# One position bias, eight table look-ups: replicating bucket numbers over partitions in TensorE or through DRAM

## The chip, the cores and the metric

The kernel runs on one core of a Trainium2 chip. The metric is the time of one execution in microseconds of device time (us), as the median of several runs. TensorE multiplies matrices, VectorE and ScalarE work element by element, GpSimd does small work on the side, and SyncE (SP) issues all the transfers of this kernel.

## The reference

Two blocks of two layers each are run one behind the other on a sequence of 512 positions and a width of 1024. Only the first block has a position bias. Its sliding-window attention adds to each score of query q and key k a number that depends on the head and on a bucket of their distance:

```python
def t5_bucket(rel):
    n = jnp.maximum(rel, 0)
    max_exact = N_BUCKETS // 2
    nf = jnp.maximum(n, max_exact).astype(jnp.float32)
    large = max_exact + (jnp.log(nf / max_exact) / math.log(MAX_DISTANCE / max_exact)
                         * (N_BUCKETS - max_exact)).astype(jnp.int32)
    return jnp.where(n < max_exact, n, jnp.minimum(large, N_BUCKETS - 1))
...
    bucket = t5_bucket(pq[..., :, None] - pk[..., None, :])
    bias = rel_bias[bucket]
```

There are 32 buckets and 8 heads. The bias is computed once, and both layers of the first block use it. The rest of the reference (latent attention, a convolution branch, gates, MLPs, and the whole second block) is not touched by the change.

## The kernel before, in words

The program is written as Python generators, one for each piece of work. `weave` (L178) takes the next step of whichever generator is furthest behind its share, so the program order of a stage is a mixture of several pieces; the number given with each piece is the count of steps that it is taken to have. From that program order a planner makes the order of each engine's and of the SP queue's instructions before the run. On the chip each engine and SP then work through their own list in that order.

`prep_bias` (L387 to L462) runs once, in layer 0, woven in `mix_first` (L535 to L537) with the latent attention `mla` (36 steps), with `inputs` (projections, 13.7 steps) and with the convolution beside them. It is entered with BIAS_STEPS = 39.7 and has 38 steps. It has four parts:

1. The distances of 128 consecutive windows are formed and turned into bucket numbers by 15 comparisons on VectorE (L415). The result is cast to bf16 as `bkr` (L420): on partition p are the buckets of one distance pattern, 512 columns wide.
2. The bias table in DRAM, `biasD` (4 blocks, 8 heads, 128 queries, 256 keys), is filled with a large negative number (L410).
3. The 32 x 8 table of bias values is split in three bf16 parts `rb` (L427), so that three matmuls give it at full precision.
4. For i from 0 to 7 (L436) and j from 0 to 3, four matmuls (L442) each copy one row of `bkr` to 32 partitions of a PSUM tile: the stationary operand is one column of the identity, repeated 32 times. The tile is compared with the partition's bucket number. For even j VectorE does this in one operation (L451), for odd j ScalarE in two (L448, L449). The result is the one-hot `oh`, and three matmuls (L454) multiply it with the parts of the table into 32 partitions of `pb`, which is one of the two PSUM banks named "sc". After four j, ScalarE copies `pb` to SBUF (L457) and SP stores it with four transfers into the diagonals of `biasD` (L461).

The one-hot comes from the tag "y1" of 8 buffers, which the latent attention's operands use too, and the replicated tile from the bank named "m", of which there is one. The scores of `mla` (L740) take their banks from "sc" as well.

What stands around it: `load_w` (L211) loads a weight tile with one transfer on SP (L222) into one of two raw buffers, ScalarE rounds it (L223) and VectorE subtracts for the low part (L224); TensorE multiplies in triples (L230, L231, L232). `softmax_causal` (L761 to L775) runs on VectorE and ScalarE. When the stage is over, the window attention `swa` loads one block of the bias at a time (L790) into the tile "bias", and adds it to its scores (L796, L798) in the tile "S". "bias" and "S" have one buffer each.

Of the kernel before, what the change touches and what calls it, by code (L numbers as in the profile page):

```python
# [13 lines left out]
BF16 = mybir.dt.bfloat16  # L14
AF = mybir.ActivationFunctionType
ALU = mybir.AluOpType
# [4 lines left out]
P = 128  # L21
T = 512
# [5 lines left out]
class Build:  # L28
# [358 lines left out]
    def prep_bias(self):  # L387

        nc, A = self.nc, self.A

        ii = self.tl([P, 8, P], I32, "bias", "ii")
        pk, d = ii[:, 0:4], ii[:, 4:8]
        src = A["pos_pad"]
        nc.sync.dma_start(out=pk, in_=bass.AP(tensor=src.tensor, offset=src.offset,
                                              ap=[[1, P], [P, 4], [1, P]]))
        pq = self.sm("pq", 4, "pq", bufs=1, dt=I32)
        src = A["positions"]
        nc.sync.dma_start(out=pq, in_=bass.AP(tensor=src.tensor, offset=src.offset, ap=[[1, P], [P, 4]]))
        nc.gpsimd.tensor_tensor(out=d, in0=pq.unsqueeze(2).to_broadcast([P, 4, P]), in1=pk, op=ALU.subtract)
        fl = self.tl([P, 2, T], F32, "S", "nfbk")  # L400
        nf, bk = fl[:, 0], fl[:, 1]
        nc.vector.tensor_copy(out=nf, in_=d.rearrange("p b e -> p (b e)"))
        nc.vector.tensor_scalar(out=bk, in0=nf, scalar1=0.0, scalar2=16.0, op0=ALU.max, op1=ALU.min)

        self.biasD = self.dram.tile([4, 8, P, 256], F32, name="biasD")
        bd = self.biasD
        neg = self.ch("neg", n=256, tag="tmp")
        nc.gpsimd.memset(neg, NEG)
        for b in range(4):
            nc.sync.dma_start(out=bd[b].rearrange("h q k -> q h k"),  # L410
                              in_=neg.unsqueeze(1).to_broadcast([P, 8, 256]))
        yield
        for j in range(1, 16):
            th = math.ceil(16.0 * 8.0 ** (j / 16.0) - 1e-9)
            nc.vector.scalar_tensor_tensor(out=bk, in0=nf, scalar=float(th), in1=bk,  # L415
                                           op0=ALU.is_ge, op1=ALU.add)
            if j % 4 == 0:
                yield
        bkr = self.ch("bkr", BF16, tag="y1")
        nc.vector.tensor_copy(out=bkr, in_=bk)  # L420
        idr = self.sm("idr", P, "idr", bufs=1, dt=BF16)
        nc.vector.tensor_copy(out=idr, in_=self.ident)

        rb, rest = [], self.cvec("rbias")
        for k in range(3):
            rb.append(self.sm("rb", 32, "rb", bufs=3, dt=BF16))
            nc.vector.tensor_copy(out=rb[k], in_=rest)  # L427
            if k < 2:
                r = self.sm("rr", 32, "rr", bufs=2)
                nc.vector.tensor_tensor(out=r, in0=rest, in1=rb[k], op=ALU.subtract)  # L430
                rest = r
        yield
        nbk = self.sm("nbk", 1, "nbk", bufs=1)
        nc.vector.tensor_scalar(out=nbk, in0=self.cvec("bucket"), scalar1=-1.0, scalar2=None, op0=ALU.mult)

        for i in range(8):  # L436
            pb = self.psum("sc")
            for j in range(4):
                ps = self.psum("m")
                for g in range(4):  # L440
                    q = 32 * j + 8 * g + i
                    nc.tensor.matmul(ps[32 * g:32 * g + 32], idr[:, q:q + 1].to_broadcast([P, 32]), bkr,  # L442
                                     start=True, stop=True)
                oh = self.ch("oh", BF16, tag="y1")
                if j % 2:

                    t = self.ch("dd", tag="tmp")
                    nc.scalar.activation(out=t, in_=ps, func=AF.Square, bias=nbk)  # L448
                    nc.scalar.activation(out=oh, in_=t, func=AF.Relu, scale=-1.0, bias=self.ones[:, 0:1])  # L449
                else:  # L450
                    nc.vector.tensor_scalar(out=oh, in0=ps, scalar1=self.cvec("bucket"), scalar2=None,  # L451
                                            op0=ALU.is_equal)
                for k, w in enumerate(rb):
                    nc.tensor.matmul(pb[32 * j:32 * j + 32], w, oh, start=k == 0, stop=k == 2)  # L454
                yield
            ob = self.ch("ob", tag="tmp")
            nc.scalar.copy(out=ob, in_=pb)  # L457
            for b in range(4):
                dst = bass.AP(tensor=bd.tensor, offset=bd.offset + b * 8 * P * 256 + i * 257 + 1,
                              ap=[[8 * 257, 16], [P * 256, 8], [1, P]])  # L460
                nc.sync.dma_start(out=dst, in_=ob[:, b * P:(b + 1) * P])  # L461
        self.dump("bias", self.biasD)  # L462
# [1819 lines left out]
        "bias": 1, "S": 1}  # L2282
MOD_STEPS = 102, 70
CONV_RATE, SWA_STEPS, REST_STEPS = (0.3, 0.6, 1.45), 11.5, 18
IN_STEPS, BIAS_STEPS, CTX_STEPS = 13.7, 39.7, 12
RWB = dict(mm=3, lv=3, z=2)
GLA = dict(wide=1, ktok=1, gst=8, ghs=1, att=2, gw=4)
ODD_RATE, ODD_STEPS, OUT_STEPS = 4, 32, 40
# [223 lines left out]
```

## Time and profile before

| | |
|---|---|
| median of 3 runs | 3931.33 us (3928.62 to 3933.89) |
| profiled execution, its own time | 3927.74 us |
| its span | 3925.7 us |
| mean granted TensorE clock | 0.969 of full speed |
| TensorE busy | 3777.0 us |
| VectorE busy | 2397.6 us |
| ScalarE busy | 1741.0 us |
| GpSimd busy | 85.0 us |
| transfers on the queue of SP | 321.47 MB |

Busy time is the union of an engine's instructions. PE is the matmuls, PEld the weight loads that overlap them, DVE is VectorE, ACT ScalarE, POOL GpSimd, SP SyncE. Matmuls are pipelined, so one that is shown with 0.39 us may be followed by the next one after 0.23. A row of the timeline gives the start, the duration, the engine, the line, the operation and its operands.

### The profile page before, as it was taken

Reading aid. Unit: us, or ns where it says so; the run is one execution under the profiler, and the core shown is the slowest. Engines: PE = TensorE matmul, PEld = TensorE weight load, DVE = VectorE, ACT = ScalarE, POOL = GpSimd, SP = SyncE. Lnnn points to the kernel's source line nnn. Section 1 sums busy time; section 2 is a strip of 40 time slices with the busy share of each in tenths; the row PEclk is TensorE's granted clock in tenths of the full one; section 3 lists DMA queues with packets and bytes.
Section 4 is the critical chain, followed back from the end, with each engine's and each line's share of the span. In section 5 each row is a group of like instructions: output and inputs, shape, how many; then the busy total and the mean of one; then the engine's idle time right before and its main releaser. Section 6 shows DMA issues by size and latency. Waiting matters only on the chain.

```text
span 3925.7 us, 54880 instructions
## 1 busy us (share of the span) xinstructions
PE 3777.0 (96%) x21506; PEld 2970.5 (76%) x21506; DVE 2397.6 (61%) x4178; ACT 1741.0 (44%) x3923; POOL 85.0 (2%) x180
## 2 busy tenths in 40 slices
PE   8999999999999999999998999999999999889998
PEld 5566888886667888778885666688888887678887
DVE  7587567665786565657646566454444574756444
ACT  4655343334653333335537788432222264533332
POOL 0000000000000000000001000000000000000000
PEclk9999999999999999999998899899999999889999
DMA  3132345442132355531110000211111212012232
GB/s 129 49 92 83 101 155 180 157 143 65 56 94 85 121 166 171 187 116 45 45 43 2 2 2 2 76 56 64 65 65 65 83 50 68 6 59 95 97 97 75
DMA packets 115699, 324.98 MB, mean 83 GB/s; under 512 B 12528, under 2 KB 34032, under 8 KB 115440
## 3 DMA queue, kind: packets, MB, share of 16 engines
q1 hardware_dynamic: 115440, 321.47, 25.4%
q8 instruction: 169, 2.77, 0.3%
q14 instruction: 90, 0.74, 0.1%
HBM read 307.27 MB, written 12.58 MB: 81 GB/s over the span
## 4 chain that ended last, share of the span: by engine, by line
PE 79%; issue 11%; ACT 5%; DVE 4%; POOL 1%; DMA 0%; POOLq 0%; DVEq 0%; SPq 0%; ACTq 0%
PE ps_g L230 20%; PE ps_g L232 20%; PE ps_g L231 20%; PE ps_mm L1564 1%; PE ps_y L750 1%; ACT B L1621 1%; PE ps_sc L740 1%; PE ps_z L1531 1%; POOL r L308 1%; PE ps_y L825 1%; PE ps_sc L796 1%; PE ps_y L1236 1%; PE ps_lv L1611 1%; PE ps_sc L454 1%; PE ps_lv L1608 1%
## 5 line engine op out<-in xcount | busy, mean ns | idle before, releaser
L230 PE MATMUL ps_g<-hi,whi 128*128 128x512 f32 (+1 forms) x4464 | 1670.5, 374 | 21.2 <-ACT whi L223 13.7
L232 PE MATMUL ps_g<-hi,wlo 128*128 128x512 f32 (+1 forms) x4464 | 1654.9, 371 | 10.5 <-DVE wlo L224 10.4
L231 PE MATMUL ps_g<-lo,whi 128*128 128x512 f32 (+1 forms) x3744 | 1401.4, 374 | 2.3 <-DVE lo L954 1.8
L223 ACT CAST whi<-raw 128x1024 fp32r<-128x1024 f32 (+3 forms) x497 | 481.7, 970 | 1241.8 <-PE ps_g L231 1064.1
L230 PEld LDWEIGHTS ps_g<-hi,whi 128*128 128x128 f32 x4464 | 847.8, 190 | 190.2 <-ACT whi L223 23.8
L232 PEld LDWEIGHTS ps_g<-hi,wlo 128*128 128x128 f32 x4464 | 847.4, 190 | 166.4 <-DVE wlo L224 17.1
L231 PEld LDWEIGHTS ps_g<-lo,whi 128*128 128x128 f32 x3744 | 709.8, 190 | 135.0 <-issue 10.5
L224 DVE TENSOR_TENSOR wlo<-raw,whi 128x1024 fp32r<-128x1024 f32 (+3 forms) x497 | 557.2, 1122 | 165.7 <-ACT whi L223 160.0
L231 PE MATMUL ps_g<-x,whi 128*128 128x512 f32 (+1 forms) x720 | 253.1, 352 | 0.0
L1130 DVE SCALAR_TENSOR_TENSOR x<-ps_g,mod,x 128x512 f32<-128x512 f32 (+1 forms) x192 | 127.0, 662 | 200.3 <-PE ps_g L232 200.1
L879 DVE SCALAR_TENSOR_TENSOR macc<-mraw,cs,macc 128x1024 f32<-128x1024 f32 x140 | 175.7, 1279 | 6.8 <-DMA mraw<-in_mod_w 6.5
L638 DVE SCALAR_TENSOR_TENSOR cv<-u,taps,cv 128x512 f32<-128x512 f32 x240 | 177.1, 744 | 1.1
L1109 DVE TENSOR_SCALAR r<-ps_g 128x512 f32<-128x512 f32 x96 | 57.6, 602 | 180.3 <-PE ps_g L232 180.2
L231 PEld LDWEIGHTS ps_g<-x,whi 128*128 128x128 f32 x720 | 138.5, 192 | 16.5 <-issue 1.6
L589 DVE TENSOR_TENSOR x<-ps_g,x 128x512 f32<-128x512 f32 x64 | 44.2, 690 | 137.8 <-PE ps_g L232 137.8
L473 DVE TENSOR_TENSOR o<-ps_g,R 128x512 f32<-128x512 f32 x76 | 52.2, 689 | 114.6 <-PE ps_g L232 111.7
L1110 ACT ACTIVATE r<-r 128x512 f32<-128x512 f32 x96 | 53.4, 557 | 145.3 <-DVE r L1109 145.3
L308 POOL TENSOR_TENSOR r<-v,mhalf 128x4 f32<-128x4 f32 (+2 forms) x30 | 38.5, 1284 | 2792.5 <-DVE v L327 2135.6
L582 DVE SCALAR_TENSOR_TENSOR r<-ps_g,R 128x512 f32<-128x512 f32 x64 | 44.0, 688 | 80.9 <-PE ps_g L232 77.0
L204 DVE TENSOR_TENSOR lo<-r,hi 128x512 fp32r<-128x512 f32 x96 | 57.6, 600 | 40.7 <-ACT hi L203 40.7
L1621 ACT COPY B<-ps_lv 32x64 f32<-32x64 f32 x384 | 77.5, 202 | 6.4
L291 ACT ACTIVATE sq<-x 128x512 f32<-128x512 f32 (+1 forms) x91 | 49.1, 543 | 70.1 <-DVE x L1130 34.7
(508 smaller groups left out, 4574.3 us busy)
## 6 DMA issues: line engine op xcount, KB each, us to landing
raw<-in_l_mlp_w SPq DMA_DIRECT2D x128, 512.0 KB, 3.5
mraw<-in_mod_w SPq DMA_DIRECT2D x96, 512.0 KB, 4.5
raw<-in_w_in SPq DMA_DIRECT2D x82, 512.0 KB, 3.4
raw<-in_w_up SPq DMA_DIRECT2D x64, 512.0 KB, 3.5
raw<-in_w_down SPq DMA_DIRECT2D x64, 512.0 KB, 3.5
raw<-in_l_w_in SPq DMA_DIRECT2D x50, 512.0 KB, 3.5
raw<-in_w_branch SPq DMA_DIRECT2D x48, 256.0 KB, 2.8
bias<-biasD SPq DMA_DIRECT2D x16, 512.0 KB, 3.9
```

What stands on the lines that cost most here:

```text
L204: nc.vector.tensor_tensor(out=lo, in0=src, in1=hi.bitcast(F32), op=ALU.subtract)
L223: nc.scalar.copy(out=hi, in_=raw)
L224: nc.vector.tensor_tensor(out=lo, in0=raw, in1=hi.bitcast(F32), op=ALU.subtract)
L230: t.matmul(ps, w[0], x[0], start=start, stop=False)
L231: t.matmul(ps, w[0], x[1], start=False, stop=False)
L232: t.matmul(ps, w[1], x[0], start=False, stop=stop)
L308: self.nc.gpsimd.tensor_tensor(out=r, in0=v, in1=self.mhalf[:, :v.shape[1]], op=ALU.pow)
L638: nc.vector.scalar_tensor_tensor(out=y, in0=u[:, j:j + T], scalar=taps[:, c * 31 + j:c * 31 + j + 1], in1=y, op0=ALU.mult, op1=ALU.add)
L879: nc.vector.scalar_tensor_tensor(out=acc[s], in0=rw, scalar=self.cs[:, k, s:s + 1], in1=acc[s], op0=ALU.mult, op1=ALU.add)
L1109: nc.vector.tensor_scalar(out=t, in0=ps[s][:, :n], scalar1=0.0, scalar2=None, op0=ALU.max)
L1130: nc.vector.scalar_tensor_tensor(out=xx[c], in0=ps[:, :n], scalar=md[:, s, 5, c:c + 1], in1=xx[c], op0=ALU.mult, op1=ALU.add)
L1621: nc.scalar.copy(out=B[rows, :, j, :], in_=blocks(ps[rows, 0:64]))
```

## The change

The buckets `bkr` are stored to DRAM once. In each turn i, four loads bring rows of them back, each row spread over 32 partitions, into one tile `oh` of 128 partitions and 4 x 512 columns. The tile alternates between the tags "S" and "bias". One VectorE operation turns all of it into the one-hot in place. Twelve matmuls follow, the table's part as the outer loop and the column tile j as the inner one. The generator yields after the loads, after the comparison and after the matmuls, so it has 30 steps in place of 38; BIAS_STEPS goes from 39.7 to 31. The copy of `pb` and the four stores stay as they are.

```diff
         bkr = self.ch("bkr", BF16, tag="y1")
         nc.vector.tensor_copy(out=bkr, in_=bk)
-        idr = self.sm("idr", P, "idr", bufs=1, dt=BF16)
-        nc.vector.tensor_copy(out=idr, in_=self.ident)
+        bkD = self.dram.tile([P, T], BF16, name="bkD")
+        nc.sync.dma_start(out=bkD, in_=bkr)
...
         yield
-        nbk = self.sm("nbk", 1, "nbk", bufs=1)
-        nc.vector.tensor_scalar(out=nbk, in0=self.cvec("bucket"), scalar1=-1.0, scalar2=None, op0=ALU.mult)
 
         for i in range(8):
+            oh = self.tl([P, 4, T], BF16, ("S", "bias")[i % 2], "oh")
+            for j in range(4):
+                src = bass.AP(tensor=bkD.tensor, offset=bkD.offset + (32 * j + i) * T,
+                              ap=[[8 * T, 4], [0, 32], [1, T]])
+                nc.sync.dma_start(out=oh[:, j], in_=src)
+            yield
+            nc.vector.tensor_scalar(out=oh, in0=oh, scalar1=self.cvec("bucket"), scalar2=None, op0=ALU.is_equal)
+            yield
             pb = self.psum("sc")
-            for j in range(4):
-                ps = self.psum("m")
-                for g in range(4):
-                    q = 32 * j + 8 * g + i
-                    nc.tensor.matmul(ps[32 * g:32 * g + 32], idr[:, q:q + 1].to_broadcast([P, 32]), bkr,
-                                     start=True, stop=True)
-                oh = self.ch("oh", BF16, tag="y1")
-                if j % 2:
-
-                    t = self.ch("dd", tag="tmp")
-                    nc.scalar.activation(out=t, in_=ps, func=AF.Square, bias=nbk)
-                    nc.scalar.activation(out=oh, in_=t, func=AF.Relu, scale=-1.0, bias=self.ones[:, 0:1])
-                else:
-                    nc.vector.tensor_scalar(out=oh, in0=ps, scalar1=self.cvec("bucket"), scalar2=None,
-                                            op0=ALU.is_equal)
-                for k, w in enumerate(rb):
-                    nc.tensor.matmul(pb[32 * j:32 * j + 32], w, oh, start=k == 0, stop=k == 2)
-                yield
+            for k, w in enumerate(rb):
+                for j in range(4):
+                    nc.tensor.matmul(pb[32 * j:32 * j + 32], w, oh[:, j], start=k == 0, stop=k == 2,
+                                     skip_group_check=True)
+            yield
             ob = self.ch("ob", tag="tmp")
             nc.scalar.copy(out=ob, in_=pb)
...
-IN_STEPS, BIAS_STEPS, CTX_STEPS = 13.7, 39.7, 12
+IN_STEPS, BIAS_STEPS, CTX_STEPS = 13.7, 31, 12
```

## Rows read from the trace of the kernel before

**Rows 1.** The page's busy line: engine, busy us, share of the span, instructions.

```profile
PE 3777.0 (96%) x21506; PEld 2970.5 (76%) x21506; DVE 2397.6 (61%) x4178; ACT 1741.0 (44%) x3923; POOL 85.0 (2%) x180
```

**Rows 2.** Windows, layer 0 and 1: us; PE, PEld, DVE, ACT, POOL busy; clock, DMA.

```profile
66.10:253.10 187.00, 183.33 (x798) 102.50 (x796) 122.91 (x264) 112.15 (x267) 0.00 (x0) 0.98 0.20 58
940.90:1089.30 148.40, 141.95 (x580) 96.98 (x579) 112.24 (x252) 87.00 (x228) 0.00 (x0) 0.95 0.17 57
```

**Rows 3.** Groups of instructions, stage of layer 0: count | busy, mean ns | idle before.

```profile
L230 PE MATMUL ps_g<-hi,whi 128*128 128x512 f32 x122 | 54.0, 442 | 1.2 <-ACT whi L223 1.2
...
L454 PE MATMUL ps_sc<-oh,rb 128*32 128x512 bf16 x96 | 26.4, 382 | 0.8 <-ACT oh L449 0.8
...
L442 PE MATMUL ps_m<-bkr,idr 128*32 128x512 bf16 x124 | 15.8, 389 | 0.5 <-ACT dd L448 0.5
...
L451 DVE TENSOR_SCALAR oh<-ps_m,cv 128x512 bf16<-128x512 f32 x16 | 11.9, 746 | 10.6 <-PE ps_sc L454 8.8 <-PE ps_m L442 1.8
...
L449 ACT ACTIVATE oh<-dd,ones 128x512 bf16<-128x512 f32 x16 | 11.6, 725 | 0.8 <-PE ps_sc L454 0.6
L448 ACT ACTIVATE dd<-ps_m,nbk 128x512 f32<-128x512 f32 x16 | 11.0, 690 | 5.5 <-PE ps_m L442 5.4
```

**Rows 4.** The same groups, stage of layer 1 (940.9 to 1089.3 us).

```profile
L230 PE MATMUL ps_g<-hi,whi 128*128 128x512 f32 x122 | 53.3, 437 | 0.9 <-ACT whi L223 0.9
```

**Rows 5.** The chain of waits in the stage of layer 0 (66.1 to 253.1 us).

```profile
by line: PE ps_g L230 18.4%; PE ps_g L231 17.1%; PE ps_g L232 16.2%; PE ps_sc L454 12.3%; PE ps_y L750 10.5%; PE ps_sc L740 10.0%; PE ps_m L442 5.6%; PE ps_tr L745 5.6%; ACT pr L771 0.8%; ACT kh L732 0.7%; ACT whi L223 0.6%; ACT pT L747 0.4
```

**Rows 6.** Timeline of TensorE's matmuls, 75.9 to 77.7 us: start, duration.

```profile
75.88 0.40 PE L442 MATMUL ps_m<-bkr,idr 128*32 128x512 bf16 x4
76.21 0.50 PE L232 MATMUL ps_g<-hi,wlo 128*128 128x512 f32 x1
...
76.87 0.82 PE L454 MATMUL ps_sc<-oh,rb 128*32 128x512 bf16 x3
77.62 0.50 PE L231 MATMUL ps_g<-lo,whi 128*128 128x512 f32 x1
```

**Rows 7.** Timeline of TensorE's matmuls, 225.3 to 225.6 us.

```profile
225.36 0.39 PE L454 MATMUL ps_sc<-oh,rb 128*32 128x512 bf16 x1
225.37 0.40 PE L442 MATMUL ps_m<-bkr,idr 128*32 128x512 bf16 x3
225.59 0.60 PE L454 MATMUL ps_sc<-oh,rb 128*32 128x512 bf16 x2
```

**Rows 8.** Groups of VectorE by form, 30 to 70 us.

```profile
L224 DVE TENSOR_TENSOR wlo<-raw,whi 128x1024 fp32r<-128x1024 f32 x3 | 3.7, 1217 | 0.0
...
L384 DVE TENSOR_SCALAR ang<-ang 128x512 f32<-128x512 f32 x1 | 0.4, 417 | 0.0
```

**Rows 9.** Transfers: KB, us to landing; queue from 14.9 to 24 us; issue durations of L461.

```profile
raw<-in_w_qup SPq DMA_DIRECT2D x12, 128.0 KB, 2.0
...
biasD<-neg SPq DMA_DIRECT2D x4, 1024.0 KB, 8.5
...
q1 hardware_dynamic: 3337, 2.90, 99.9%
...
L461 SPq DMA_DIRECT2D biasD<-ob x32: 518/597/764, 89.3 to 231.5; - x32
```

**Rows 10.** Waits of SP, 55 to 235 us: total, times, longest.

```profile
SPq L222 <- DVE wlo L224: 61.9, 10, 11.1
```

**Rows 11.** The replications, over the whole run: ns min/median/max, first and last start.

```profile
L442 PE MATMUL ps_m<-bkr,idr x128: 376/389/609, 63.2 to 226.0; 128*32 128x512 bf16 x128
```

**Rows 12.** Timeline of VectorE at 49.5 us.

```profile
49.50 0.15 DVE L662 TENSOR_SCALAR bh<-cv 128x4 f32<-128x4 f32 x1
```

**Rows 13.** Timeline of SP at 232 us.

```profile
232.18 0.52 SPq L790 DMA_DIRECT2D bias<-biasD  x1
```

## The prediction

> **What bounds the kernel now.** I read the page's busy line first, to see which engine the whole run hangs on: TensorE is busy 96% of the span, VectorE 61%, ScalarE 44% [rows 1]. TensorE time that is removed can therefore come off the end, and time on the others mostly cannot. An average does not tell that of one stage, so the windows come next. The bias is built only in layer 0, beside the latent attention; the stage from the first score matmul (L740) to the first window score (L796) is 187.0 us long there, with TensorE busy 183.3 us. The same stage of layer 1, which builds no bias, takes 148.4 us [rows 2]. Its other work is the same (122 first products at L230 in both [rows 3, 4]), so this kernel contains its own control: the bias costs **38.6 us** of that stage. The lines of the stage say on what: 96 look-ups (L454) for 26.4 us, 124 of the 128 replications (L442) for 15.8 us, on VectorE 16 one-hots (L451) for 11.9 us, on ScalarE 32 more passes (L448, L449) for 22.6 us [rows 3]. The chain of waits agrees on where it hurts: L454 holds 12.3% and L442 5.6% of the stage's 187.0 us, 23.0 and 10.5, in sum **33.5 us**, and the one-hots are not among its large shares [rows 5].
>
> **What the edit saves.** All 128 replications go, with their 10.5 us of chain. The 96 look-ups stay 96 matmuls, but in eight groups of 12 over four column tiles in turn, in place of 32 groups of three on one tile. Three on one tile hold the next product back for 77.62 - 76.87 = 0.75 us; four replications on four tiles only for 76.21 - 75.88 = 0.33 us [rows 6]. So tiles overlap. Replications share one moving operand though, and the new look-ups bring four. The trace shows that too: one look-up, moving the one-hot, starts at 225.36 and three replications, moving the buckets, at 225.37, and the next look-up on the first tile comes at 225.59 as if it were alone [rows 7]. Two moving operands ran at once. I therefore price 12 as three rounds, like three in a row: 0.75 us, times 8 = **6.0 us** put back; the other end is all in series, 12 x 0.25 = 3.0 us, times 8 = 24.
>
> Against the chain this leaves 33.5 - 6.0 = 27.5 us; against the control 38.6 - 6.0 = 32.6. I take **27.5**, because eight ScalarE copies (L457), the one-hots and all the DMA of the bias remain in layer 0, and layer 1 has none of it.
>
> **What it puts in, and what hides it.**
> VectorE: 16 one-hots out of PSUM (11.9 us) become eight of 128x2048 from SBUF to SBUF. No row has that form. The nearest is the SBUF-to-SBUF scalar operation L384, 0.417 us for 512 columns, so at most four times that, 1.7 us; the ends are 0.42 and, by the two-input subtraction L224 at 1.22 us for 1024, 2.4 us [rows 8]. I take 1.7, 13.6 us in all. VectorE then carries 122.9 - 11.9 + 13.6 = 124.6 us in a stage of 187.0 - 27.5 = 159.5: 35 us idle hide it. ScalarE loses 22.6 us of 112.2 and needs no cover. The two small VectorE operations that go (the bf16 identity, the negated bucket) and the second score bank that comes free earlier count for nothing of their own: the control has both already.
>
> SP: one store and 32 loads are new. The bias stores L461, also issued four at a time, took 0.60 us each [rows 9]: 2.4 us for the four of a look-up, 19 us in all. SP has room, since it stood 61.9 us waiting at L222 for a weight buffer alone [rows 10]. Behind these issues stand the weight loads and the stores of the bias. The store of the buckets also waits for the cast L420, and the first load for the store to land; at 2.0 us for 128 KB that holds SP once, before the place of the first replication, with two weight buffers to draw on. Each later load waits for the matmuls that read its tile two turns before; those are long done. Cost on the path: nothing, at worst the 2.4 us of one set of issues for each look-up, 19 us, if SP were late with weights all eight times.
>
> The wait that is new is VectorE's, for the four loads. Behind it on VectorE stand the low halves of the weights (L224), which TensorE needs, and the softmax reductions. A 128-row load of 1 KB a row, the shape of each new one, lands in 2.0 us; the 1 KB rows that fill the bias in DRAM are the slow end, 8.5 us [rows 9]. The last of four is issued 1.8 us after the first, so it lands after 3.8 to 10.3 us. The weave gives cover: the 32 groups of replications start from 63.2 to 226.0 us [rows 11], one step of prep_bias each 163 / 31 = 5.3 us; with 31 steps in place of 39.7 over the shortened stage that is 5.3 x 39.7 / 31 x 159.5 / 187 = 5.8 us. Covered at 3.8, 4.5 us short at 10.3. But the queues do not keep the program's order: a preparation of the layer norm that the program reaches only after the bias (L662) runs at 49.50 us [rows 12], so the one-hot can come up on VectorE sooner than a step later. I take the near row, 2.0 us, and no exposed wait. At the far end eight waits of 10.3 us, 82 us, are more than the idle 35; that is the rival on the other side.
>
> The end of the bias: its last store is issued at 231.5 us [rows 9] and the first load of it at 232.18 [rows 13], some 21 us before the first window scores, which end the stage at 253.1 [rows 2]. prep_bias ends at step 30 of 31 in place of 38 of 39.7, the same place; this margin covers one longer look-up.
>
> **The sum.** The profiled execution took 3927.7 us (span 3925.7 and 2.0 around it), 3.6 below the median of the runs, 3931.3. 3927.7 - 27.5 = 3900.2, and on the scale of the median **3904**.
>
> **Rivals.**
> *Loads crowd onto few engines.* Each new load's source has an outer dimension of only 4 (the other 32 rows repeat). If its packets then use four of the 16 DMA engines, four loads put 128 packets on each of these. While the bias was filled, 2.90 MB took 99.9% of 16 engines for 9.1 us, 145.5 us of engine time, so one engine needs 51 ns for a KB [rows 9]: 6.5 us, and with the 2.0 of a landing 8.5. Past a step of 5.8 us that is 2.7 us of VectorE wait eight times, 22 us; without cover 68 us; midway 45 us, somewhat above the idle 35. I let a quarter of it, 11 us, come through to TensorE, which has a product or two queued: 3915. For it: the pattern in the diff. Against: two buffers let SP load early, and the waiting stays off TensorE in part.
> The Trainium skill's page "DMA: Bandwidth & Descriptors", section "Why a DMA increments its semaphore by 16 and not by 1", says that a transfer is spread over the largest number of engines up to 16 that divides the slowest dimension of both sides, here 4. By this rule the time is 3915, by the nearest row 3904; the rows above are of transfers whose outer dimension is 16 or 128, so the trace of before neither supports nor denies it.
>
> *The column tiles do not overlap* (the change does not do what it says). 24 us are put back: 33.5 - 24 = 9.5 us gained, 3922. The two moving operands at 225.4 us speak against it [rows 7].
>
> *The gain is lost elsewhere.* A new order on every queue, or the softmax, takes it. The control, which has the softmax without the bias, speaks against it: about 3931.
>
> *Slower: VectorE becomes the bound.* It stands in order at each one-hot with L224 behind it. The stage is as long as before once 124.6 + 8w = 187.0, at a wait w of 7.8 us for each look-up. At the far end w is 10.3 and the stage 124.6 + 82 = 207 us, 20 longer: 3951. For it: 8.5 us has been seen. Against: that was with 1 MB transfers in a row, and it needs no cover at all.
>
> **Chances.** Forecast 0.55, few engines 0.27, no overlap 0.05, lost 0.08, slower 0.05. The forecast's own range goes from 38.6 gained (3893) to about 20 (3911); the few-engines case from 3911 to 3920; **3893 to 3920** over both leaves out the no-overlap case, the lost, the slower, and the edges. About 0.2%, 8 us, is what a measurement of this kernel can tell: the first three cases are faster, 0.87; lost is the same, 0.08; slower 0.05.
>
> **What would show it.** In the changed profile: no L442; groups of 12 look-ups that hold the next product for 0.75 us (2 or more: no overlap); a stage of about 160 us between the first L740 and L796; a one-hot of 0.4 to 2.4 us. VectorE's wait for the loads should be under 2 us each; 3 to 8 us and landings of 7 or more mean few engines. The forecast is wrong if the stage stays over 175 us, and wrong in its reason if the stage shrinks and gives the time back before the first window scores, waiting for the bias.

## The result, and the profile after

The changed kernel took **3967.74 us** (median of 4 runs, 3963.77 to 3970.83), the kernel before 3930.62 beside it: ratio 1.0099, 95% interval 1.0085 to 1.0113. The forecast was 3904 and the range ended at 3920: the change is slower where I expected it to be faster. The profiled execution took 3963.77 us, its span is 3961.9.

The busy line of the page and the two windows of [rows 1, 2], now for the kernel after (stage of layer 0, then of layer 1; columns as there):

```profile
PE 3780.7 (95%) x21378; PEld 2966.7 (75%) x21378; DVE 2391.9 (60%) x4168; ACT 1721.3 (43%) x3891; POOL 85.6 (2%) x180
```

```profile
64.70:262.30 197.60, 167.43 (x678) 105.74 (x678) 118.09 (x260) 93.89 (x237) 0.00 (x0) 0.86 0.27 77
967.30:1113.50 146.20, 139.84 (x580) 95.38 (x579) 112.31 (x252) 87.03 (x228) 0.00 (x0) 0.98 0.18 58
```

TensorE has 128 instructions fewer in the run and is busy 3.7 us *longer* than in [rows 1]. In the stage with the bias it is busy 15.9 us less than in [rows 2], and the stage is 10.6 us longer all the same: idle time went from 187.0 - 183.3 = 3.7 us to 197.6 - 167.4 = 30.2, and the mean granted clock from 0.98 to 0.86. The layer-1 control is close to what it was (148.4 and 146.2 us). So the work did leave, and something worse came. The groups of the stage and its chain of waits say what:

```profile
L441 DVE TENSOR_SCALAR oh<-oh,cv 128x2048 bf16<-128x2048 bf16 x8 | 6.0, 753 | 34.2 <-DMA oh<-bkD 24.8 <-DMA raw<-in_w_kup 5.2 <-DMA raw<-in_w_qup 4.3
L446 PE MATMUL ps_sc<-oh,rb 128*32 128x512 bf16 x96 | 7.3, 413 | 0.0
```

```profile
by line: DMA oh<-bkD 17.5%; PE ps_g L230 10.2%; PE ps_g L232 10.1%; PE ps_g L231 10.0%; PE ps_y L743 9.3%; SPq L439 6.7%; PE ps_sc L733 5.8%; SPq L454 5.2%; PE ps_tr L738 4.8%; DMA raw<-in_w_kup 2.9%; PE ps_sc L446 2.7%; DMA raw<-in_w_qup 2
```

The 96 look-ups fell from 26.4 us busy [rows 3] to 7.3. The eight one-hots take 0.75 us each. But VectorE stands 34.2 us in front of them, and the loads lead the chain with 17.5%, where [rows 5] had no transfer at all. One of the eight episodes, in the timeline of all engines (start, duration, engine, line; in brackets the idle time before and what ended it):

```profile
98.73 2.68 SPq L439 DMA_DIRECT2D oh<-bkD  x4
...
109.83 0.75 DVE L441 TENSOR_SCALAR oh<-oh,cv 128x2048 bf16<-128x2048 bf16 x1 [5.31 <-DMA oh<-bkD]
110.50 0.16 DVE L766 RECIPROCAL rec<-sum 128x1 f32<-128x1 f32 x1
110.69 0.61 ACT L767 ACTIVATE pr<-pr,rec 128x384 f32<-128x384 f32 x1 [5.11 <-DVE rec L766]
...
111.36 0.90 PE L738 MATMUL ps_tr<-ident,pr 128*128 128x128 f32 x3 [4.99 <-ACT pr L767]
```

The loads are issued at 98.73 and the one-hot can start at 109.83, 11.1 us later. A reciprocal of the softmax (L766) stands behind it on VectorE, ScalarE waits for that, and TensorE for ScalarE. Over the whole stage (65 to 262 us), this last wait is the longest of TensorE's (total, times, longest), 18.5 of its 30.2 us of idle time:

```profile
PE ps_tr L738 <- ACT pr L767: 18.5, 7, 5.3
```

The windows around the episode (columns as in [rows 2]):

```profile
98.70:103.70 5.00, 4.98 (x22) 3.15 (x21) 4.05 (x11) 2.69 (x8) 0.00 (x0) 1.00 0.26 76
103.70:106.70 3.00, 2.67 (x21) 1.42 (x19) 0.82 (x3) 1.23 (x3) 0.00 (x0) 1.00 0.97 146
106.70:108.70 2.00, 0.00 (x0) 0.00 (x0) 0.00 (x0) 0.00 (x0) 0.00 (x0) 1.00 0.46 103
108.70:111.70 3.00, 0.34 (x2) 0.35 (x3) 1.87 (x4) 0.99 (x2) 0.00 (x0) 0.51 0.26 92
111.70:115.70 4.00, 1.35 (x5) 0.65 (x3) 3.25 (x8) 3.90 (x10) 0.00 (x0) 0.50 0.27 90
```

The DMA share is 0.26 while the loads run alone, about four of 16 engines (from 103.7 to 106.7 us a weight load, issued at 103.20, runs beside them), and once TensorE has stood still from 106.7 us its granted clock is 0.5 (1.2 GHz) from 108.7 on, so the matmuls after the wait are slow as well.

That is a quarter of the loss. The first window score (L789) comes at 262.29 instead of 253.1 us, 9 us late; the end comes 36 us late. The other 27 us are there when the second block begins. They build up evenly through the rest of the first block, 1,500 us in which nothing was edited: the first product of macc and sel starts at 590.15 us before and 606.56 after, 16.4 us late, and the first product of x, where the second block begins, at 1737.02 and 1776.07, 39.1 late. The second block adds nothing (36.2 late at its end). There is no wait there; the matmuls themselves follow each other more slowly. TensorE's timeline in the layer-0 MLP, before and then after, eight gaps each:

```profile
599.70 0.39 PE L230 MATMUL ps_g<-hi,whi 128*128 128x512 f32 x1
...
601.52 0.39 PE L232 MATMUL ps_g<-hi,wlo 128*128 128x512 f32 x1
```

```profile
599.70 0.40 PE L231 MATMUL ps_g<-lo,whi 128*128 128x512 f32 x1
...
601.56 0.40 PE L230 MATMUL ps_g<-hi,whi 128*128 128x512 f32 x1
```

1.82 us against 1.86, at a granted clock of 1.00 in both. Over all neighbouring products between 600 and 900 us the median distance is 0.227 us before and 0.235 after; the whole MLP stretch takes 404.5 and 415.4 us, filled with matmuls in both. What differs is where the tiles lie: the change drops two small tiles, idr (256 bytes) and nbk (32), from the pool at the bottom of the first block's memory, and every tile allocated behind them moves down by 288 bytes. By the allocation of the programs as built, weights begin 96 bytes into a 128-byte line in both kernels; the moving operands begin at 96 before and at 64 after.

### The profile page after: what moved, and what is told of

The parts are those of the page before. It is cut to its first block, busy times and chain, and to the rows that moved or that the text cites. A ratio compares the mean times of both kernels' runs of the same rounds, so it can differ in the third digit from the quotient of the medians.

```text
span 3961.9 us, 54607 instructions
## 1 busy us (share of the span) xinstructions
PE 3780.7 (95%) x21378; PEld 2966.7 (75%) x21378; DVE 2391.9 (60%) x4168; ACT 1721.3 (43%) x3891; POOL 85.6 (2%) x180
## 4 chain that ended last, share of the span: by engine, by line
PE 77%; issue 11%; ACT 5%; DVE 4%; POOL 1%; DMA 1%; SPq 1%; POOLq 0%; DVEq 0%; ACTq 0%
PE ps_g L230 20%; PE ps_g L232 20%; PE ps_g L231 20%; PE ps_mm L1557 1%; PE ps_y L743 1%; ACT B L1614 1%; DMA oh<-bkD 1%; POOL r L308 1%; PE ps_z L1524 1%; PE ps_sc L733 1%; PE ps_y L818 1%; PE ps_sc L789 1%; PE ps_y L1229 1%; PE ps_g L2152 1%; PE ps_lv L1604 1%
## 5 line engine op out<-in xcount | busy, mean ns | idle before, releaser
L230 PE MATMUL ps_g<-hi,whi 128*128 128x512 f32 (+1 forms) x4464 | 1678.5, 376 | 22.1 <-ACT whi L223 14.6
L232 PE MATMUL ps_g<-hi,wlo 128*128 128x512 f32 (+1 forms) x4464 | 1663.8, 373 | 12.1 <-DVE wlo L224 11.9
L230 PEld LDWEIGHTS ps_g<-hi,whi 128*128 128x128 f32 x4464 | 847.5, 190 | 196.3 <-ACT whi L223 25.2
L232 PEld LDWEIGHTS ps_g<-hi,wlo 128*128 128x128 f32 x4464 | 846.6, 190 | 180.5 <-DVE wlo L224 21.5
L224 DVE TENSOR_TENSOR wlo<-raw,whi 128x1024 fp32r<-128x1024 f32 (+3 forms) x497 | 557.4, 1122 | 165.7 <-ACT whi L223 160.9
```

Of the source, the lines that this page charges most:

```text
L224: nc.vector.tensor_tensor(out=lo, in0=raw, in1=hi.bitcast(F32), op=ALU.subtract)
L230: t.matmul(ps, w[0], x[0], start=start, stop=False)
L232: t.matmul(ps, w[1], x[0], start=False, stop=stop)
```

## The experiments

Two theories, then: the loads of the buckets are carried by four engines and land late; and the operands' addresses slow every first-block product. Each was undone alone, then both. All ratios are to runs of the kernel before on the same chip in the same session. "Stage" is the window from the first recorded latent score to the first window score (66.5 to 253.1 us before, 0.4 shorter than in [rows 2]), "L230" the mean duration of that product between 500 and 890 us.

| run | median us | ratio (95%) | stage us, clock | L230 ns |
|---|---|---|---|---|
| before | 3930.62 | 1 | 186.6, 0.98 | 391 |
| after | 3967.74 | 1.0099 (1.0085 to 1.0113) | 197.6, 0.86 | 397 |
| e1 after, 32-byte tile | 3939.63 | 1.0012 (0.9997 to 1.0027) | 191.8, 0.89 | 391 |
| e2 after, 64-byte tile | 3970.09 | 1.0090 (1.0073 to 1.0107) | 191.6, 0.89 | 397 |
| e3 before, 32-byte tile | 3962.62 | 1.0069 (1.0053 to 1.0085) | 186.3, 0.99 | 397 |
| e4 loads over 16 engines | 3943.71 | 1.0023 (1.0007 to 1.0038) | 165.7, 0.93 | 397 |
| e5 e4 and 32-byte tile | 3907.32 | 0.9952 (0.9937 to 0.9967) | 165.1, 0.93 | 391 |
| e6 e4, weights shifted | 3906.51 | 0.9955 (0.9939 to 0.9971) | 164.6, 0.93 | 391 |
| e7 before, 64-byte tile | 3937.51 | 1.0034 (1.0023 to 1.0045) | 185.9, 0.99 | 393 |
| e8 before, 12 look-ups | 3910.0 | 0.9953 (0.9937 to 0.9969) | 169.7, 0.97 | 391 |
| e9 e5, look-ups in series | 3911.27 | 0.9965 (0.9953 to 0.9977) | 163.5, 0.94 | 391 |
| e10 e5, second block moved | 3907.7 | 0.9954 (0.9937 to 0.9971) | 163.2, 0.95 | 391 |
| e11 e5, look-ups in threes | 3915.53 | 0.9952 (0.9934 to 0.9970) | 166.7, 0.96 | 392 |
| e12 e5, nine more look-ups | 3916.21 | 0.9972 (0.9961 to 0.9983) | 171.7, 0.98 | 391 |

### Addresses: e1, e2, e3

```diff
+        pad = self.sm("pad", 8, "pad", bufs=1)
+        nc.gpsimd.memset(pad, 0.0)
```

This stands at the head of prep_bias, in the kernel after (e1), there with 16 columns in place of 8 (e2), and in the kernel before (e3).

> The kernel after, with one more 32-byte tile ahead of the first block's tiles, so that every later tile of that block lies 32 bytes higher, as far into a 64-byte line as in the kernel before (the change took out two small tiles, 288 bytes together). Theory A (addresses): about 27 of the 37 us lost come from matmuls whose moving operand begins on a multiple of 64 bytes and that then follow each other every 0.2333 us instead of every 0.2268 us; the pad takes them back: 3938 to 3944 us, and the L230 matmuls of the layer-0 MLP have a mean of about 391 ns again. Rival B (order of work or the clock behind the bias stage is the cause): no change, 3964 to 3971 us and a mean of about 397 ns. Both: the bias stage itself stays at about 197 us with some 34 us of VectorE waits for the loads.

> The control of the run above: a 64-byte tile instead of the 32-byte one. Everything is moved, but the addresses stay as they are within a 64-byte line. Theory A (addresses modulo 64): no change, 3964 to 3971 us, L230 in the layer-0 MLP at about 397 ns. Rival (any extra tile and its memset, or addresses in some larger unit): as the 32-byte run, 3938 to 3944 us.

> The kernel before with the same 32-byte tile and nothing else: its first block's moving operands then begin on multiples of 64 bytes. Theory A: the loss without the change, 3955 to 3962 us, with the matmuls of the layer-0 MLP at 0.233 us and L230 there at about 397 ns. Rival B: 3928 to 3934 us.

All three came out as the address theory has it, with two small misses: e3 ended 0.6 us above its range, and the stage of e1 took 191.8 us where about 197 was expected. The group of L230 between 500 and 890 us, in the kernel after, in e1 and in e3:

```profile
L230 PE MATMUL ps_g<-hi,whi 128*128 128x512 f32 x543 | 215.6, 397 | 0.0
```

```profile
L230 PE MATMUL ps_g<-hi,whi 128*128 128x512 f32 x558 | 218.1, 391 | 0.0
```

```profile
L230 PE MATMUL ps_g<-hi,whi 128*128 128x512 f32 x541 | 214.9, 397 | 0.0
```

An unused tile of 32 bytes makes the kernel after 0.87% faster (1.0099 to 1.0012, 34 us), one of 64 bytes does nothing, and the same 32 bytes make the kernel **before** 0.69% slower with no other edit. So this loss has nothing to do with how the bias is computed: it came with two tiles that were no longer needed.

### Loads: e4, and both mends: e5

```diff
-            for j in range(4):
-                src = bass.AP(tensor=bkD.tensor, offset=bkD.offset + (32 * j + i) * T,
-                              ap=[[8 * T, 4], [0, 32], [1, T]])
-                nc.sync.dma_start(out=oh[:, j], in_=src)
+            for g in range(4):
+                src = bass.AP(tensor=bkD.tensor, offset=bkD.offset + (8 * g + i) * T,
+                              ap=[[0, 32], [32 * T, 4], [1, T]])
+                nc.sync.dma_start(out=oh[32 * g:32 * g + 32], in_=src)
```

The same rows go to the same places, in as many transfers of as many bytes; only the repeat of 32 is now the outermost dimension, ahead of the four rows.

> The kernel after with each of the four loads filling 32 partitions by four tiles instead of 128 partitions by one tile from a source that repeats in the middle; the data are the same. Theory C (the loads are carried by four of the sixteen DMA engines, and this makes them land late): with the repeat outermost all engines carry them, the loads land in 2 to 4 us, VectorE's waits for oh fall from 34 us to under 10, the bias stage from 197.6 to 160 to 172 us with its clock back above 0.93, and the time to 3932 to 3945 us (the addresses are left as in the kernel after). Rival D (the landing is late because of the queue's order or the issue on SP, or the stage is long for another reason): the landing stays above 6 us and the time at 3960 to 3970 us.

The packet counts tell of the engines, if each transfer adds one small packet per engine that takes part. Before, after and e4, first line of the DMA part of each page:

```profile
DMA packets 115699, 324.98 MB, mean 83 GB/s; under 512 B 12528, under 2 KB 34032, under 8 KB 115440
```

```profile
DMA packets 120066, 329.29 MB, mean 83 GB/s; under 512 B 12672, under 2 KB 38400, under 8 KB 119808
```

```profile
DMA packets 120450, 329.29 MB, mean 84 GB/s; under 512 B 13056, under 2 KB 38784, under 8 KB 120192
```

Under 512 B the kernel after has 144 more than before, 16 for the store and 32 x 4 for the loads; e4 has 528 more, 16 + 32 x 16. The Trainium skill's rule, cited in the prediction, that the slowest dimension sets the number of engines (page "DMA: Bandwidth & Descriptors", section "Why a DMA increments its semaphore by 16 and not by 1"), agrees with both. What it did to the wait: group and window of e4, TensorE's wait for the softmax, the chain of the stage, and the loads' median time from issue to landing (the last figure):

```profile
L441 DVE TENSOR_SCALAR oh<-oh,cv 128x2048 bf16<-128x2048 bf16 x8 | 6.0, 749 | 3.5 <-DMA oh<-bkD 3.5
```

```profile
65.30:231.00 165.70, 155.15 (x677) 100.50 (x678) 117.98 (x259) 93.00 (x237) 0.00 (x0) 0.93 0.37 92
```

```profile
PE ps_tr L738 <- ACT pr L767: 1.1, 1, 1.1
```

```profile
by line: PE ps_g L230 16.3%; PE ps_g L232 16.2%; PE ps_g L231 15.7%; PE ps_y L743 12.5%; PE ps_sc L733 9.8%; PE ps_tr L738 5.2%; DMA oh<-bkD 4.2%; PE ps_sc L446 3.6%; ACT whi L223 2.4%; issue 1.4%; ACT kh L725 1.4%; SPq L454 1.4%; ACT pr L7
```

```profile
oh<-bkD SPq DMA_DIRECT2D x32, 128.0 KB, 5.6
```

VectorE's wait falls from 34.2 to 3.5 us, TensorE's wait for the softmax behind it from 18.5 to 1.1, and the stage from 197.6 to 165.7. Of these 31.9 us, TensorE's idle time is 30.2 - 10.6 = 19.6, and the other 12.3 are the same matmuls (678 and 677 of them) busy for 167.4 us at a clock of 0.86 and for 155.2 at 0.93. The first theory of the loads holds, but for the landing: 2 to 4 us were expected and 5.6 measured. Of the rival, the issue falls: SP issues as many transfers, and L439 and L454, which had 6.7% and 5.2% of the chain in the kernel after, are down to 1.4% for L454, with L439 no longer among the large shares. The order of the queue is not excluded as strictly, because in e4 some of the loads stand a few places elsewhere in it; the packet counts and the DMA share of 0.26 speak for the engines.

> Both mended at once: the loads over 16 DMA engines (as in the run loads16, which took the time from 3967.7 to 3943.7 us and the first read of the bias from 262.3 to 231.0 us) and the 32-byte tile (which took it from 3967.7 to 3939.6 us). Theory: the two are independent, so 3943.7 - 28.1 = 3915.6 us, range 3902 to 3920 (the stretch of the second block from about 2260 to 2540 us took 266 us in some profiles and 280 us in others, with its granted clock between 0.94 and 0.86, and I cannot say beforehand which it will be); the first read of the bias at 228 to 232 us, the L230 matmuls of the layer-0 MLP at about 391 ns. Rival: the two share a cause (both gains come out of the clock behind the bias stage): 3935 to 3943 us.

3907.32 us. The pad is worth 34 us without the new loads and 28 with them (1.0023 to 0.9952), the loads 30 without the pad (1.0099 to 1.0023) and 24 with it (1.0012 to 0.9952). Each ratio is known to about 6 us on either side, so the two pairs agree: within that, these are two independent losses, and with both mended the change does what it was forecast to do in kind: 0.48% faster than before, 18.9 us, where 27.5 were forecast. This version beats both kernels.

### Which address counts: e6, e7, e10

```diff
+        pad = self.xp.tile([P, 8], F32, tag="xpad", name="xpad", bufs=1)
+        nc.gpsimd.memset(pad, 0.0)
```

For e6 this stands ahead of the first tile of the residual stream in the kernel of e4, and moves the weights instead; e7 is e3 with 16 columns.

> As loads16, but instead of the moving operands the weights are moved: a 32-byte tile ahead of the residual stream shifts the weight pool of the first block by 32 bytes, so that weights and moving operands both begin 64 bytes into a 128-byte line (in the kernel before both begin at 96; in the kernel after the moving operands at 64 and the weights at 96). Theory A1 (what counts is that weights and moving operands lie alike in a line): the matmuls of the layer-0 MLP at 0.227 us and L230 there at about 391 ns, 3902 to 3920 us, as with the 32-byte tile. Theory A2 (what counts is where the moving operand alone begins): 0.233 to 0.235 us, about 397 ns, 3940 to 3947 us, as in loads16.

> The kernel before with a 64-byte tile: the first block's moving operands begin at 32 in a 128-byte line, the weights at 96, so they are alike within 64 bytes and unlike within 128. If 64 bytes count: as the kernel before, 3925 to 3936 us, L230 in the layer-0 MLP at 391 ns. If 128 bytes count: slow matmuls, 397 ns, 3953 to 3966 us. For the second speaks that the MLP of the second block's first layer runs at 0.233 us in every profile and has its operands at 32 against 96.

e6 is as fast as e5: with weights and moving operands both at 64, products are 0.227 us apart again. In the first block no address of a moving operand was changed from the slow e4, only those of the weights, so it is not the moving operand's place alone that counts; that the two lie alike is what fits all the runs. A rival is left untested: no run has weights at 64 with the moving operands of the MLP elsewhere, so weights at 64 might be fast with any of them. e7 lies between the two expectations: at 32 against 96, alike in 64 bytes and unlike in 128, the products are 0.229 us apart and the kernel is 0.34% slower than before, half of what e3 lost. In sum, by the median distance in the layer-0 MLP: 0.227 us for 96/96 and 64/64; 0.229 for 32/96; 0.234 to 0.235 for 0/96 and 64/96 (moving / weights, bytes into a 128-byte line).

e10 asks the same of another place: on top of e5, a tile ahead of the second block's first layer.

```diff
+            pad = self.sm("pad", 16, "pad", bufs=1)
+            self.nc.gpsimd.memset(pad, 0.0)
             x, xc, px, accs = self.layer_even(x, accs, px, self.md[0], stages)
```

> The kernel with both mends and, in the second block's first layer, one more 64-byte tile ahead of its tiles, which takes the moving operands of that layer's MLP from 32 to 96 in a 128-byte line, as the weights lie. Theory A1 (alike in a line is fast): the 512-column matmuls between 2500 and 3100 us go from 0.231 - 0.235 us apart to about 0.227; some 1,600 of them by 4 to 8 ns: 6 to 13 us less, 3893 to 3903 us. Rival: that layer's matmuls are slow for another reason (512 and 256 columns take turns there): the spacing stays, and the time at 3902 to 3912 us.

A miss, and an instructive one: the time is the rival's, but the spacing did move. Groups of L230 from 2560 to 3080 us, in e5 and then in e10:

```profile
L230 PE MATMUL ps_g<-hi,whi 128*128 128x512 f32 x492 | 195.0, 396 | 1.0 <-ACT hi L948 0.6 <-ACT whi L223 0.4
L230 PE MATMUL ps_g<-hi,whi 128*128 128x256 f32 x492 | 136.1, 277 | 0.0
```

```profile
L230 PE MATMUL ps_g<-hi,whi 128*128 128x512 f32 x492 | 193.3, 393 | 0.0
L230 PE MATMUL ps_g<-hi,whi 128*128 128x256 f32 x492 | 138.6, 282 | 0.0
```

The 512-column products became faster as expected (median distance 0.231 to 0.227 us), and the 256-column products that take turns with them slower by more (0.113 to 0.120). The layer gained nothing. So "alike in a line" is a rule for 512 columns with these weights, not for all shapes; what the memory or TensorE does there stays open.

### What the change itself is worth: e8, e9, e11, e12

e8 makes one part of the change alone. TensorE still repeats the buckets; the one-hots of a group go into one tile, and its look-ups follow together:

```diff
+            oh4 = self.tl([P, 4, T], BF16, ("S", "bias")[i % 2], "oh")
...
-                oh = self.ch("oh", BF16, tag="y1")
+                oh = oh4[:, j]
...
-                for k, w in enumerate(rb):
-                    nc.tensor.matmul(pb[32 * j:32 * j + 32], w, oh, start=k == 0, stop=k == 2)
-                yield
+                yield
+            for k, w in enumerate(rb):
+                for j in range(4):
+                    nc.tensor.matmul(pb[32 * j:32 * j + 32], w, oh4[:, j], start=k == 0, stop=k == 2,
+                                     skip_group_check=True)
```

> The kernel before with one part of the change alone: the bucket rows are still repeated by TensorE and compared by VectorE and ScalarE, but the four one-hot tiles of a group are kept and its 12 look-ups follow each other, alternating over the four column tiles. Theory (the look-ups in threes were on the path, 23.0 us of the stage by the chain, and cost 0.83 us for 12 as the kernel after shows): the stage shrinks by 23.0 - 6.6 = 16 us and the time falls to 3910 to 3918 us. Rival (TensorE would have waited for the one-hot tiles anyway): the stage stays within 4 us and the time at 3926 to 3934 us. All the small tiles stay, so no address in the first block's pools moves in either case.

As the theory had it: 3910.0 us, the stage 17 us shorter. But it is as fast as e5, which also has the buckets from DRAM and TensorE 128 repeats fewer (ratios 0.9953 and 0.9952). The windows of e8 and of e5:

```profile
65.40:235.10 169.70, 164.27 (x797) 98.96 (x795) 122.14 (x264) 111.48 (x267) 0.00 (x0) 0.97 0.22 62
```

```profile
67.80:232.90 165.10, 154.52 (x677) 99.89 (x677) 117.69 (x259) 92.81 (x237) 0.00 (x0) 0.93 0.40 92
```

TensorE is busy 9.8 us less in e5 and the stage is 4.6 us shorter: idle time doubles, 5.4 to 10.6 us, and the clock falls.

e9 swaps two loop lines of e5, so that the three look-ups of a column tile follow each other:

```diff
-            for k, w in enumerate(rb):
-                for j in range(4):
+            for j in range(4):
+                for k, w in enumerate(rb):
```

> The other part of the change alone, on the kernel with both mends (3907.3 us): the buckets come through DRAM as there, but the 12 look-ups of a group go column tile by column tile, the three of a tile behind each other, as in the kernel before. Theory (the gain is the column tiles' overlap, and the DRAM path gives next to nothing: the kernel before with the regrouped look-ups alone took 3910.0 us): 12 look-ups take 3.0 us instead of 0.83, so 8 x 2.2 = 17 us come back in the bias stage: 3920 to 3928 us, about the time of the kernel before. Rival (the repeats that TensorE no longer makes were on the path too, and the tiles' order is of little weight): 3905 to 3914 us.

The time lies in the rival's range, and the order is indeed of little weight. But neither expectation names the reason. TensorE's timeline of e9 at one group,

```profile
118.42 0.85 PE L448 MATMUL ps_sc<-oh,rb 128*32 128x512 bf16 x12
119.20 0.50 PE L230 MATMUL ps_g<-hi,whi 128*128 128x512 f32 x1
```

shows 12 look-ups in series of three holding TensorE for 0.78 us, as in alternation (0.76). In the single records four start together, 0.010 us apart, then four more 0.216 us later: the first look-up of the second column tile starts beside the first of the first tile, ahead of the two that stand before it in the program. The column tiles behave as if each worked off its own queue. The kernel before shows the same by name:

```profile
226.02 0.38 PE L442 MATMUL ps_m<-bkr,idr 128*32 128x512 bf16 x1
```

In the program as built, the three look-ups of [rows 7], all on one column tile, stand ahead of the four replications. Three of these start at 225.37 all the same, before the second look-up at 225.59, and the fourth, which goes to the look-ups' own column tile, only here, when they are through. Alternating the tiles is not needed; standing next to each other is.

e11 adds a yield after each column tile's three look-ups (and the steps for it to the planner, 55 for 31), so that other work may come between them, as before.

```diff
                 for k, w in enumerate(rb):
...
+                yield
-            yield
```

> What pays, after the run series showed that 12 look-ups take 0.83 us in either order: here the buckets come through DRAM over 16 engines with the 32-byte tile, but the main flow of matmuls may come between the look-ups of one column tile and those of the next, as in the kernel before (three look-ups on one column tile, then other work). Theory G (a column tile works off its own queue, so look-ups overlap only where those of several tiles stand behind each other in the program; the grouping is the whole gain): threes hold TensorE for 0.75 us each, 24.0 - 6.6 = 17 us come back, less where the planner still sets threes next to each other: 3916 to 3927 us, the first read of the bias at 243 to 252 us. Rival D (the DRAM path is worth something by itself, 128 repeats of buckets fewer on TensorE): half of the chain's 10.5 us or more remains, 3908 to 3915 us.

Inconclusive for its question. The planner let other matmuls in only here and there:

```profile
127.85 0.82 PE L448 MATMUL ps_sc<-oh,rb 128*32 128x512 bf16 x3
128.60 0.50 PE L231 MATMUL ps_g<-lo,whi 128*128 128x512 f32 x1
...
138.79 0.84 PE L448 MATMUL ps_sc<-oh,rb 128*32 128x512 bf16 x9
139.56 0.33 PE L740 MATMUL ps_tr<-ident,pr 128*128 128x128 f32 x1
```

Three look-ups hold TensorE 0.75 us, and nine 0.77, which fits the reading of the queues. But the look-ups held it 14.8 us in all instead of 24, and the stage grew by 1.6 us only, far from the 243 us that theory G gave for its end (230.1). The ratio is that of e5. That leaves the question why TensorE time has become so cheap, which e12 asks directly:

```diff
+            for more in range(9):
+                nc.tensor.matmul(pb[0:32], rb[0], oh[:, more % 4], start=False, stop=True, skip_group_check=True)
```

> What a microsecond of TensorE is worth in this stage, now that part of its time is idle: the kernel with both mends (3907.3 us) with nine more look-ups behind the 12 of every group, all on the first column tile, so that they stand in one queue and cannot overlap: 9 x 0.216 = 1.94 us per group, 15.6 us in all (they add to the first tile's sums, so the bias of a quarter of the diagonals comes out different). Theory S (TensorE now waits for ScalarE and VectorE for 12 us of the stage, so its time has no full price any more, and this is why removing 33 us of it brought 20): the stage grows by 4 to 10 us, 3911 to 3917 us. Rival (every TensorE microsecond of the stage is on the path): 14 to 17 us more, 3921 to 3926 us. By either the 21 look-ups of a group hold TensorE for about 2.8 us; if they hold it for 0.83 us or so, look-ups on one column tile do overlap and the reading of the queues is wrong.

```profile
123.15 0.83 PE L448 MATMUL ps_sc<-oh,rb 128*32 128x512 bf16 x12
123.81 2.11 PE L451 MATMUL ps_sc<-oh,rb 128*32 128x512 bf16 x9
125.84 0.49 PE L737 MATMUL ps_sc<-kh,qh 96*128 96x128 f32 x2
```

```profile
65.00:236.70 171.70, 164.05 (x749) 103.56 (x749) 120.59 (x260) 93.34 (x237) 0.00 (x0) 0.98 0.39 88
```

A group of 21 holds TensorE 125.84 - 123.15 = 2.69 us, nine on one tile are in series. Over the eight groups the hold rises from 7.4 to 22.5 us, by 15.1, the stage by 171.7 - 165.1 = 6.6 us, and the time by 0.20%, 8 us. Theory S has the time: in the mended kernel a microsecond of TensorE added to this stage costs 0.44 us of the stage. Its reason, the waits, has the smaller part. Beside e5's window above, idle time fell only from 10.6 to 7.7 us, 2.9 of the missing 8.5. TensorE is busy 164.05 - 154.52 = 9.5 us more, where 15.1 were put in, so the other matmuls, 581 in both windows, took some 5.6 us less: the granted clock is 0.98 in this window and 0.93 in e5's. e11's window has 0.96. That the added work keeps the clock up is a reading of these windows; no run holds the clock and changes the work.

What TensorE waits for in the mended kernel stands in e5's waits from 64 to 233 us (total, times, longest):

```profile
PE ps_g L230 <- ACT whi L223: 4.6, 4, 2.2
PE ps_sc L735 <- ACT kh L727: 3.8, 2, 2.5
PE ps_y L745 <- ACT pT L742: 2.0, 2, 1.1
```

These are ScalarE's casts of the weights, of the keys and of the probabilities. In the kernel before, L230 waited 1.2 us for the weights in the stage [rows 3], so some cover that the bias work had given them seems to be gone.

## Why the prediction was wrong

**Right: what the look-ups cost.** The 0.75 us for 12 look-ups was measured as 0.76, the tiles overlap with two or more moving operands, and the rival "no overlap" is out. The order of the tiles in the loop, with the column tile as the inner one, makes next to no difference (e9). The one-hot, priced at 1.7 us, took 0.75.

**Right in kind, mis-sized: the saving.** 27.5 us forecast; with both mends the stage is 21.5 us shorter (186.6 to 165.1) and the kernel 18.9 us faster. I took the chain's shares of L454 and L442 [rows 5] to be fully removable. They are not, together: e8 takes away the look-ups' time and gains 17 us of stage, which is the chain's 23.0 less 6.0; taking the repeats as well gains 4.6 more where the chain had 10.5, and this is the term that was mis-sized. TensorE's busy time fell by 28.4 us (182.9 in the window of 186.6, to 154.5 in e5), about as forecast, but its idle time rose by 6.9, from 3.7 to 10.6.

**Wrong: "I take the near row, 2.0 us, and no exposed wait."** This is the first step that failed. The near row reads 128 separate source rows [rows 9]; the new loads have its tile and its bytes and ran on four engines. The shape of the tile was the wrong likeness, the outermost dimension of the source the right one. Even over 16 engines the loads took a median of 5.6 us to land (e4) and not 2.0, close to the 5.8 of cover, and two of the eight one-hots still waited, 3.5 us together. The rival of the few engines had this and was the right mechanism at a wrong price: I gave four loads 8.5 us and let a quarter of 45 us through, 11 us. They took 11.1 us in the episode shown, and the loss was 24 to 30 us, since the waiting one-hot held the softmax's reciprocal (which I had named as standing behind it) and TensorE's clock then fell: 12.3 of the stage's 31.9 us are matmuls at the lower clock, which no term of mine held. The condition for the slower rival, a wait of 7.8 us for each look-up, was not met (34.2 / 8 = 4.3 us), and VectorE was busy only 118.1 us of 197.6: it was not the bound, it was late.

Two statements on SP beside it failed too. The matmuls that read a load's tile two turns before were to be "long done"; in the kernel after, SP stood waiting for them (total, times, longest, 55 to 235 us):

```profile
SPq L439 <- PE ps_sc L446: 24.6, 4, 9.4
```

The issues were to cost nothing on the path, and L439 and L454 had 11.9% of the stage's chain, 23.5 us. With the loads on 16 engines L454 is left with 1.4%, though SP still waits 15.1 us for look-ups: the issues were on the path because the loads were late.

**Wrong: the two small operations that go "count for nothing of their own".** This step cost 28 to 34 us, as much as the loads or more. I looked at the time of the bf16 identity and of the negated bucket, and not at their 288 bytes. The control that I trusted could not show it: layer 1 of the kernel before has neither operation, but it lies in the same program and its operands at the same addresses. Nothing in the profile of before could have priced it, but the second block's products at a median of 0.232 us (2560 to 3080 us) beside the first block's 0.227, in the same trace, show that the spacing is not a constant of the form.

**What stays open.** Why the addresses matter, and the rule for other shapes (e10) and for weights elsewhere than at 96. Whether the clock would have stayed up in e5 with other work in the gaps. What the DRAM path is worth with look-ups strictly in threes (e11 did not make them so); what e5 and e8 show is that on top of grouped look-ups it shortens the stage by 4.6 us and brings nothing that can be measured in the time.

## What to carry to other kernels

When an edit adds or drops a tile, however small, compare the distance of untouched matmuls far from the edit: here 288 bytes cost more than the edit gained once both losses were mended, and a 32-byte pad took it back. When a row is spread over partitions by a transfer, put the large dimension outermost on both sides (here the repeat of 32 in place of the four rows), and count the small packets to see how many engines carry it. Matmuls on different column tiles overlap wherever they stand together, in any order; ask what else is late, and what the granted clock will do, before adding up the time of two cuts in one stage.

## What the runs showed of the hardware

- Products of 512 fp32r columns follow each other every 0.227 us when weights and moving operand begin alike within a 128-byte line, and every 0.229 to 0.235 us when they do not (e1 to e7; the addresses are those of the programs as built); products of 256 columns went the other way, 0.113 to 0.120 (e10).
- Four transfers of 128 KB on four engines were complete 11.1 us after the first issue, with the DMA share at 0.26 while they ran alone and a weight load beside them for some 3 us.
- Column tiles behave as if each had a queue of its own: three look-ups on one tile hold TensorE for 0.75 us, 12 on four tiles for 0.76 to 0.78 in either order, 21 with nine more on one tile for 2.69.
- One unedited stretch of the second block takes 266 or 280 us from one profile to the next, with its granted clock, here in the kernel before and in e4; so stages were compared beside whole times:

```profile
2258.60:2525.10 266.50, 246.86 (x2913) 164.03 (x2913) 164.33 (x450) 199.52 (x791) 11.64 (x14) 0.93 0.08 24
```

```profile
2260.10:2540.30 280.20, 260.71 (x2912) 171.47 (x2912) 164.69 (x450) 200.24 (x791) 11.66 (x14) 0.87 0.07 23
```
